# A transformer step on one Trainium2 core: the first stage loads x by tokens, turns it on TensorE, and has its order written by hand

## The chip, the cores and the metric

The kernel runs on one core of a Trainium2 chip. The metric is the device time of one execution in microseconds (us), as the median of several runs. The profile is one execution with the hardware profiler on. Engines are named as the profile names them: PE is TensorE (PEld its weight loads), DVE is VectorE, ACT is ScalarE, POOL is GpSimd, SP is SyncE, which here only issues DMAs.

## The reference, cut to what matters

One step of a two-layer model on 384 tokens of width 1024: 128 context tokens and 256 latent tokens. What the change touches is the start of the first layer, up to the attention's values:

```
def rmsnorm(x, g):
    y = xf * lax.rsqrt(jnp.mean(xf * xf, axis=-1, keepdims=True) + EPS)
    return (y * g)
mod = jax.nn.silu(cond) @ w_ada + b_ada        # six vectors: sm, cm, gm, sf, cf, gf
h = modulate(rmsnorm(x, norm_mix_g[l]), sm, cm) # h * (1 + scale) + shift
q, k, v = qkv_proj(h, w_qkv[j])                # here: v = h @ w_v
```

Context and latent tokens have different conditioning vectors, so shift and scale differ between the two groups. After it come keys, queries, attention, the output projection, a gated convolutional FFN, a second layer with a spatial gMLP, and its FFN.

## The kernel before, in words

Activations lie with features on partitions: `x[0..7]` are eight tiles of 128 features by 384 tokens. Each float32 product is made of three products of a rounded and a rest part (`mac`, L101 to L105: hi·hi, lo·hi, hi·lo). The parts of a weight tile `st` are made on ACT (`hi`, a cast) and DVE (`lo`, the difference).

The first stage, "values' stage", begins at the start of the program and ends with the first product of the keys. In it:

- SP loads x as eight pieces of 128x384 (L66), already turned on the host; then per feature block k two tiles `adw` of modulation weights (512 KB each) and a tile `st` of value weights (512 KB). `adw` has four buffers, `st` three.
- ACT squares each piece of x, DVE adds them up (`square`, L267 to L272), PE sums over partitions (`sums`, L284), DVE and POOL make r = 1/rms (`rsqrt`), and PE spreads r over the partitions into `R` (`rms`, L302).
- `ada_block(k)` (L145 to L157) makes shift and scale of feature block k: 16 small products into a bank, a copy on ACT to `ada_sb`, a turn by PE (L151), three small steps on DVE.
- `modulated` (L328 to L332) makes block k of h in two parts: `u` (named t384, shown as t) = x·scale·R on DVE, `hhi` on ACT, `hlo` on DVE, each for 128 and then 256 tokens.
- Per block k, 18 products of 128x512 add V into six banks `acc`, one for each half of the width and each of three blocks of tokens.

```
        acc = [bank(q) for q in (ps_mm, ps_mm, ps_mm, ps_sc, ps_sc, ps_ta)]
        for k in range(KD):
            modulated(0, SM, CM, k, R)
            w = load(w_v[k])
            if k < KD - 1:
                ada_block(k + 1)
```

PE starts with 18 products of a tile of ones, which nothing reads (L80). In this stage a scheduler sets the order of instructions on each engine. Behind it (from L580 to L663 of the function `attention`) the order of PE, ACT, DVE and SP is the one in which the code is written; from the fifth output tile on a scheduler sets it again.

Of the kernel before, what the change touches and what calls it, by code (L numbers as in the profile page):

```python
# [8 lines left out]
F32 = mybir.dt.float32  # L9
# [6 lines left out]
P = 128  # L16
# [23 lines left out]
def backbone(ctx: ExitStack, tc: tile.TileContext, xT_in, cond_in, condr_in, b_ada_in, prm_in,  # L40
# [17 lines left out]
    def bank(pool):  # L58
        return pool.tile([P, 512], F32, name="bank", tag="bank")


    cond = cst.tile([P, KD, 2], F32, name="cond")
    nc.gpsimd.dma_start(cond, cond_in)
    x = [cst.tile([P, NT], F32, name=f"x{k}") for k in range(KD)]
# [4 lines left out]
    nc.scalar.activation(zero, zero, AF.Silu)  # L69
    cond_s = cst.tile([P, KD, 32], F32, name="cond_s")  # L70
    nc.vector.memset(cond_s, 0.0)
    nc.scalar.activation(cond_s[:, :, 0:2], cond, AF.Silu)
# [49 lines left out]
    def ada_load(f):  # L122
# [7 lines left out]
    w_first = ada_load(0)  # L130
    b_ada = cst.tile([P, 2, 48], F32, name="b_ada")
    nc.sync.dma_start(b_ada, b_ada_in)
    prm = cst.tile([P, NPRM], F32, name="prm")
    nc.sync.dma_start(prm, prm_in)

    def ada_block(f, tpool=ps_tb):


        pa = bank(ps_ad)
        w = ada_load(f) if f else w_first  # L140
# [9 lines left out]
        tp = bank(tpool)  # L150
# [144 lines left out]
    def rms(ss=None, pin=False):  # L295

        if ss is None:
            ss = sums()
        r = inverse(ss)
        R = bank(ps_tb)  # L300
        for b in range(3):
            mm = nc.tensor.matmul(R[:, b * P:(b + 1) * P], r[:, b:b + 1].to_broadcast([P, P]), ident,  # L302
                                  start=True, stop=True)
            if pin and b == 0:
                tc.keep_in_program_order(mm)
        return R
# [64 lines left out]
    def h(k, s=slice(0, NT)):  # L371
        return hhi[:, k, s], hlo[:, k, s]
# [15 lines left out]
    def attention(pool, wkp):  # L388
# [23 lines left out]
        acc = [bank(q) for q in (ps_mm, ps_mm, ps_mm, ps_sc, ps_sc, ps_ta)]  # L412
        for k in range(KD):
            modulated(0, SM, CM, k, R)
            w = load(w_v[k])
            if k < KD - 1:
                ada_block(k + 1)
            for half in range(2):
                for b in range(3):
                    mac(acc[3 * half + b], h(k, slice(b * P, (b + 1) * P)),  # L420
                        wsel(w, half, slice(0, 512)), k == 0, k == KD - 1)
        for b in range(3):
            for half in range(2):
                nc.scalar.copy(V[:, b, 512 * half:512 * half + 512], acc[3 * half + b])
        nc.gpsimd.dma_start(sv_out, V[:, 0, :])

        allm = slice(0, P)
# [134 lines left out]
        def values(t, pT, pool=ps_mm):  # L562
# [11 lines left out]
            for hh in range(2):  # L574
# [5 lines left out]
        order = tc.manual_schedule(engines={mybir.EngineType.PE, mybir.EngineType.Activation,  # L580
                                            mybir.EngineType.DVE, mybir.EngineType.SP})
        order.__enter__()
# [5 lines left out]
        ready()  # L588
        p = products()
        ready()  # L590
# [72 lines left out]
        order.__exit__(None, None, None)  # L663
# [185 lines left out]
def _layout(inp):  # L849
# [8 lines left out]
    xT = xx.T.reshape(KD, P, NT).transpose(1, 0, 2)  # L858
# [8 lines left out]
    def units(w):  # L867
# [9 lines left out]
        "xT": xT, "cond": cond, "condr": np.stack([A["c_ctx"], A["c"][0]]),  # L877
# [39 lines left out]
```

## Time and profile before

| | |
|---|---|
| median of 3 runs | 1020.77 us (1020.12 to 1022.55) |
| profiled execution, its own time | 1021.07 us |
| its span in the trace | 1019.3 us |
| PE busy | 997.6 us, 98% of the span |
| DVE, ACT, POOL busy | 775.9, 482.0, 14.7 us |
| mean granted clock of PE | 0.991 of full speed |
| mean DMA rate | 170 GB/s |

The span runs from the first to the last instruction of the trace; the execution's own time is 1.8 us longer. Busy shares are averages over the whole program: what a change to the first stage can bring is read from that stage alone.

### The profile page before, as it was taken

To read this page: it belongs to the slowest core of one execution; us is meant where nothing else is said; L and a number is where in the kernel's file an instruction comes from. 1 tells how busy PE (TensorE), PEld (TensorE's weight loads), DVE (VectorE), ACT (ScalarE), POOL (GpSimd) and SP (SyncE) were. 2 spreads that over 40 slices of the span, in tenths; PEclk is the share of its full clock that TensorE was granted. 3 is DMA by queue.
4 is the path that set the end of the run, shared out by engine and by line. 5 is a ranking of instruction groups with operands and counts; after the bars stand their busy time and mean duration, and the time that the engine had idled before them with its cause. 6 is when DMAs were issued, how large, how long until landed. Compare 5 with 4: busy or idle time off the path is not lost.

```text
span 1019.3 us, 15937 instructions
## 1 busy us (share of the span) xinstructions
PE 997.6 (98%) x6012; PEld 947.1 (93%) x6012; DVE 775.9 (76%) x1591; ACT 482.0 (47%) x841; POOL 14.7 (1%) x29
## 2 busy tenths in 40 slices
PE   7999999999999999999999999999999999999996
PEld 6788788789999999999998889999999999999996
DVE  3646666568999898999989999688598777776652
ACT  3446555557655555433354434343385444443331
POOL 1000000000000000000000000000000000000000
PEclk7999999999999999999999999999999999999998
DMA  7874646624465555576737765565325434435521
GB/s 261 303 251 147 211 153 220 230 83 146 136 191 169 165 147 159 149 240 203 227 116 258 240 210 154 172 206 187 104 84 166 144 124 125 124 114 172 159 72 62
DMA packets 53933, 172.96 MB, mean 170 GB/s; under 512 B 6225, under 2 KB 12513, under 8 KB 53857
## 3 DMA queue, kind: packets, MB, share of 16 engines
q1 hardware_dynamic: 52992, 170.11, 51.8%
q8 instruction: 47, 0.77, 0.3%
q0 software_dynamic: 432, 1.06, 0.3%
q10 hardware_dynamic: 432, 0.79, 0.2%
q14 instruction: 30, 0.24, 0.1%
HBM read 169.31 MB, written 2.62 MB: 169 GB/s over the span
## 4 chain that ended last, share of the span: by engine, by line
PE 91%; DMA 3%; DVE 2%; ACT 2%; issue 1%; POOL 0%; SPq 0%; POOLq 0%; ACTq 0%; DVEq 0%
PE bank L103 28%; PE bank L105 28%; PE bank L104 28%; DMA kT<-in_ckT 2%; PE bank L145 1%; PE bank L788 1%; PE bank L568 1%; PE bank L519 1%; PE bank L190 1%; PE bank L551 1%; DMA adw<-in_w_ada 1%; PE bank L284 1%; ACT pr L536 0%; DMA cond<-in_cond 0%; PE bank L302 0%
## 5 line engine op out<-in xcount | busy, mean ns | idle before, releaser
L96 ACT CAST hi<-st 128x1024 fp32r<-128x1024 f32 (+1 forms) x192 | 198.1, 1033 | 300.6 <-PE bank L104 239.0
L105 PE MATMUL bank<-hhi,lo 128*128 128x384 f32 (+1 forms) x960 | 325.2, 339 | 0.2 <-DVE lo L109 0.2
L104 PE MATMUL bank<-hlo,hi 128*128 128x384 f32 (+1 forms) x960 | 324.7, 338 | 0.0
L103 PE MATMUL bank<-hhi,hi 128*128 128x384 f32 (+1 forms) x960 | 324.6, 338 | 0.0
L97 DVE TENSOR_TENSOR lo<-st,hi 128x1024 fp32r<-128x1024 f32 (+1 forms) x192 | 230.0, 1199 | 66.4 <-ACT hi L96 66.1
L105 PEld LDWEIGHTS bank<-hhi,lo 128*128 128x128 f32 x960 | 181.1, 189 | 0.5 <-DVE lo L109 0.5
L103 PEld LDWEIGHTS bank<-hhi,hi 128*128 128x128 f32 x960 | 181.0, 189 | 0.4 <-ACT kT L475 0.2
L104 PEld LDWEIGHTS bank<-hlo,hi 128*128 128x128 f32 x960 | 180.4, 188 | 0.1
L248 DVE CUSTOM_DVE_ANT_0 junk<-adw,cs 128x1024 bf16<-128x1024 f32 x112 | 136.6, 1219 | 1.0
L105 PE MATMUL bank<-ahi,lo 128*128 128x384 f32 x352 | 118.9, 338 | 0.0
L104 PE MATMUL bank<-alo,hi 128*128 128x384 f32 x352 | 118.9, 338 | 0.0
L103 PE MATMUL bank<-ahi,hi 128*128 128x384 f32 x352 | 118.7, 338 | 0.0
L105 PEld LDWEIGHTS bank<-ahi,lo 128*128 128x128 f32 x352 | 66.1, 188 | 0.0
L104 PEld LDWEIGHTS bank<-alo,hi 128*128 128x128 f32 x352 | 66.1, 188 | 0.0
L103 PEld LDWEIGHTS bank<-ahi,hi 128*128 128x128 f32 x352 | 66.1, 188 | 0.0
L103 PE MATMUL bank<-hi,hhi 128*128 128x512 f32 x144 | 58.2, 408 | 1.8 <-ACT hhi L330 1.8
L104 PE MATMUL bank<-lo,hhi 128*128 128x512 f32 x144 | 57.4, 398 | 0.0
L105 PE MATMUL bank<-hi,hlo 128*128 128x512 f32 x144 | 57.3, 399 | 0.0
L376 DVE SCALAR_TENSOR_TENSOR x<-bank,mod,x 128x128 f32<-128x128 f32 x64 | 23.8, 412 | 34.4 <-PE bank L105 34.2
L103 PE MATMUL bank<-mhi,hi 128*128 128x384 f32 x128 | 43.3, 339 | 0.0
L105 PE MATMUL bank<-mhi,lo 128*128 128x384 f32 x128 | 43.2, 337 | 0.0
L104 PE MATMUL bank<-mlo,hi 128*128 128x384 f32 x128 | 43.1, 337 | 0.0
(154 smaller groups left out, 1265.5 us busy)
## 6 DMA issues: line engine op xcount, KB each, us to landing
st<-in_w_up SPq DMA_DIRECT2D x88, 512.0 KB, 3.6
adw<-in_w_adaT SPq DMA_DIRECT2D x56, 512.0 KB, 4.2
adw<-in_w_ada SPq DMA_DIRECT2D x40, 512.0 KB, 5.6
st<-in_w_down SPq DMA_DIRECT2D x32, 512.0 KB, 3.6
st<-in_w_qk SPq DMA_DIRECT2D x16, 512.0 KB, 3.7
st<-in_w_gu SPq DMA_DIRECT2D x16, 512.0 KB, 4.3
st<-in_w_gv SPq DMA_DIRECT2D x16, 512.0 KB, 4.5
st<-in_w_gout SPq DMA_DIRECT2D x16, 512.0 KB, 4.5
```

What stands on the lines that cost most here:

```text
L96: nc.scalar.copy(hi[:, :n], st[:, :n])
L97: nc.vector.tensor_tensor(lo[:, :n], st[:, :n], hi[:, :n].bitcast(F32), ALU.subtract)
L103: nc.tensor.matmul(out, a[0], b[0], start=start, stop=False)
L104: nc.tensor.matmul(out, a[0], b[1], start=False, stop=False)
L105: nc.tensor.matmul(out, a[1], b[0], start=False, stop=stop)
L145: nc.tensor.matmul(pa[32 * j:32 * j + 32, 0:P], cond_s[:, 4 * hf + kk, :], w[hf][:, kk, P * q:P * q + P], start=(kk == 0), stop=(kk == 3), ...
L190: nc.tensor.matmul(self.pa[32 * j:32 * j + 32, 0:256], cond_s[:, k, :], t[:, 256 * j:256 * j + 256], start=(k == 0), stop=(k == KD - 1), t ...
L248: tc.keep_in_program_order(nc.vector.tensor_tensor_reduce(self.junk, t, self.cs[c], 1.0, 0.0, ALU.mult, ALU.add, m[:, c:c + 1]))
L284: mm = nc.tensor.matmul(ss[:, 2 * b:2 * b + 2], src[:, b * P:(b + 1) * P], ones[:, 0:2], start=(i == 0 and b == 0), stop=(i == len(srcs) - ...
L376: nc.vector.scalar_tensor_tensor(x[m][:, a:b], ps[:, a:b], mod(l, gate, m, c), x[m][:, a:b], ALU.mult, ALU.add)
L519: nc.tensor.matmul(sc[hh][:, cols], q[qp][HS[hh], qs:qs + P], k[kp][HS[hh], ks], start=i == 0, stop=i == 2)
L551: nc.tensor.transpose((ta[:, o:o + P] if g < 2 else tb[:, o - 512:o - 512 + P]), pr[:, b, g * P:g * P + P], ident)
```

## The change

- x comes as three tiles of 128 tokens by 1024 features (`xs`, in three buffers of the pool of `lo` tiles, which the order rows name `lo`). The first and third are issued by SP, the second by ACT. PE turns them (`turn_x`, 24 turns of 128x128 into the banks of `acc`), ACT and DVE copy the eight results to `x[k]` (`copy_x`).
- The sum of squares is taken along each token's row, by one instruction for each tile (ACT twice, DVE once); `sums` is not called here any more. R is used from its bank for block 0 and copied afterwards.
- `b_ada` and `prm` (small parameter tiles) are loaded by POOL in place of SP, behind `cond` and before `ident` is made.
- The second pair of `adw` tiles (`late=True`) is first touched by a memset on DVE, placed behind the last step of r; its loads wait for that, and the loads behind them in SP's queue too. Later pairs are issued three blocks ahead.
- PE is given 8 products of a constant bfloat16 tile `fill` at the start in place of the 18 of ones, one more behind each tile's turns, 4 before R and 5 before the first product of V (`busy`).
- The whole stage is under the written order. In block k, the weights of block k+1 are split at the start of the step; the modulation products of block k+1 stand behind the first of six groups of three products, and their turn behind the second.
- The last block's products stand behind the first loads of the keys' stage, and V's six copies out are shared: four on ACT and two on DVE.

```diff
+    xs = [wlp.tile([P, D], F32R, name="lo", tag="lo").bitcast(F32) for _ in range(3)]
+    for b in range(3):
+        (nc.sync, nc.scalar)[b % 2].dma_start(xs[b], x_in[b])
-    for k in range(KD):
-        nc.sync.dma_start(x[k], xT_in[:, k, :])
-    warm = bank(ps_ad)
-    for _ in range(18):
-        nc.tensor.matmul(warm[:, :P], ones, ones, start=True, stop=True)
+            if late:
+                nc.vector.memset(st[:, 0:1], 0.0)
-        for k in range(KD):
-            square(k, ("t384", "t384", "R0")[k % 3])
-        ss = sums(True)
-        ada_block(0, ps_ta)
-        Rp = rms(ss, True)
+        aw = {0: ada_load(0)}
+        st = [v_load(0)]
+        busy(8, idle)
+        for b in range(3):
+            if b == 1:
+                nc.vector.tensor_tensor_reduce(jv, xs[b], xs[b], 1.0, 0.0, ALU.mult, ALU.add, ssq[:, b:b + 1])
+            else:
+                nc.scalar.activation(junk, xs[b], AF.Square, accum_out=ssq[:, b:b + 1])
+            for k in range(6):
+                turn_x(k, acc[k], (b,))
+            busy(1, idle)
+        r = rsqrt(ssq[:, 0:3], tmp.tile([P, 4], F32, name="rv", tag="rv", bufs=2)[:, 0:3], 1.0 / D)
+        aw[1] = ada_load(1, True)
+        st.append(v_load(1))
+        for k in range(6):
+            copy_x(k, acc[k])
+        busy(4, idle)
+        Rp = spread(r)
+        sb = ada_products(aw.pop(0))
+        aw[2] = ada_load(2)
+        st.append(v_load(2))
+        for k in (6, 7):
+            turn_x(k, acc[k - 2], range(3))
+        w = v_high(st.pop(0))
+        ada_turned(0, sb, acc[5][:, NT:512])
+        shaped(0, Rp, lambda: v_low(w, 0, 512))
...
+        v_low(w, 512, 1024)
+        busy(5, acc[3])
+        for k in range(KD - 1):
+            if k:
+                w2 = v_high(st.pop(0))
+                v_low(w2)
+            v_part(k, w, parts[:1])
+            sb = ada_products(aw.pop(k + 1))
+            if k + 3 < KD:
+                aw[k + 3] = ada_load(k + 3)
+                st.append(v_load(k + 3))
+            v_part(k, w, parts[1:2])
+            ada_turned(k + 1, sb, bank(ps_tb))
+            if not k:
+                w2 = v_high(st.pop(0))
+            shaped(k + 1, R, None if k else lambda: v_low(w2))
+            v_part(k, w, parts[2:])
+            w = w2
```

PE, from its start to the second block of modulation products, before (`ones` is the tile of ones; a name's number is the buffer's):

```order
L80 MATMUL bank<-ones 128x128 x18
L284 MATMUL bank<-ones,sqacc 128x2 x3
L284 MATMUL bank<-ones,t_213 128x2 x3
L145 MATMUL bank<-adw,cond_s 32x128 x16
L151 MATMUL bank<-ident,ada_sb 128x128
L302 MATMUL bank<-ident,rr 128x128 x3
L103 MATMUL bank<-hi,hhi 128x512 x2
L145 MATMUL bank<-adw,cond_s 32x128 x2
L103 MATMUL bank<-hi,hhi 128x512 x2
L104 MATMUL bank<-lo,hhi 128x512
```

PE after the change, from the turns of the third tile of x (`lo` is that tile) to the same place; the rows left out are fills:

```order
L449 MATMUL bank<-ident,lo 128x128 x6
L417 LDWEIGHTS fill
L417 MATMUL bank<-fill 128x512
...
L310 MATMUL bank<-ident,rr 128x128 x3
L150 MATMUL bank<-adw,cond_s 32x128 x16
L449 MATMUL bank<-ident,lo 128x128 x6
L158 MATMUL bank<-ident,ada_sb 128x128
...
L112 MATMUL bank<-hi,hhi 128x512
L113 MATMUL bank<-lo,hhi 128x512
L114 MATMUL bank<-hi,hlo 128x512
L150 MATMUL bank<-adw,cond_s 32x128 x16
```

The sums over partitions are gone, R now stands ahead of the first modulation products, six turns of x stand between those and their own turn, and the first V group is complete (hi·hi, lo·hi, hi·lo) before the next modulation block.

DVE before, from the first step of r to the first `hlo`:

```order
L311 TENSOR_SCALAR rv<-bank 128x3
L315 TENSOR_TENSOR rt<-ry 128x3
L316 SCALAR_TENSOR_TENSOR rt<-rt,rv 128x3
L318 SCALAR_TENSOR_TENSOR rr<-rt,ry 128x3
L154 TENSOR_TENSOR mod_143<-bank,b_ada 128x2x2
L157 TENSOR_TENSOR mod_143<-mod_143,bank 128x2x2
L117 SCALAR_TENSOR_TENSOR mod_143<-mod_143,prm 128x2
L328 SCALAR_TENSOR_TENSOR t_267<-x_93,mod_143,R_259 128x128
L328 SCALAR_TENSOR_TENSOR t_267<-x_93,mod_143,R_259 128x256
L97 TENSOR_TENSOR lo<-st,hi 128x1024
L332 SCALAR_TENSOR_TENSOR hlo<-t_267,mod_143,hhi 128x128
```

DVE after, from the last step of r on:

```order
L324 SCALAR_TENSOR_TENSOR rr<-rt,ry 128x3
L137 MEMSET adw 128x1 x2
L452 COPY x_99<-bank 128x384
L452 COPY x_101<-bank 128x384
L452 COPY x_103<-bank 128x384
L161 TENSOR_TENSOR mod_129<-bank,b_ada 128x2x2
L164 TENSOR_TENSOR mod_129<-mod_129,bank 128x2x2
L126 SCALAR_TENSOR_TENSOR mod_129<-mod_129,prm 128x2
L438 SCALAR_TENSOR_TENSOR t_289<-x_99,mod_129,bank 128x128
L438 SCALAR_TENSOR_TENSOR t_289<-x_99,mod_129,bank 128x256
L432 TENSOR_TENSOR lo<-st,hi 128x512
L444 SCALAR_TENSOR_TENSOR hlo<-t_289,mod_129,hhi 128x128
```

The two memsets that release the second pair of `adw` loads, and three copies of x, now stand between r and the modulation, and only the first half of `lo` stands ahead of `hlo`.

SP before, from the last piece of x:

```order
L66 DMA x_100<-in_xT 128x384
L127 DMA adw<-in_w_ada 128x1024 x2
L132 DMA b_ada<-in_b_ada 128x96
L134 DMA prm<-in_prm 128x408
L93 DMA st<-in_w_v 128x1024
L127 DMA adw<-in_w_ada 128x1024 x2
L93 DMA st<-in_w_v 128x1024
```

SP after, from its start (`lo` are the first and third tile of x):

```order
L71 DMA lo<-in_x 128x1024 x2
L139 DMA adw<-in_w_ada 128x1024 x2
L421 DMA st<-in_w_v 128x1024
L139 DMA adw<-in_w_ada 128x1024 x2
L421 DMA st<-in_w_v 128x1024
```

Eight pieces became two on this queue, the small parameters left it, and the fourth row here waits for DVE's memsets, with everything behind it.

## Rows read from the trace of the kernel before

**Rows 1.** The page, part 1: busy time and share of the span, instructions.

```profile
PE 997.6 (98%) x6012; PEld 947.1 (93%) x6012; DVE 775.9 (76%) x1591; ACT 482.0 (47%) x841; POOL 14.7 (1%) x29
```

**Rows 2.** Stretch by engine: length, busy time (count) each, granted clock, DMA share, GB/s.

```profile
18.00:65.00 47.00, 46.98 (x375) 34.03 (x376) 25.64 (x61) 19.86 (x36) 0.27 (x1) 0.94 0.75 259
```

**Rows 3.** Timeline of 0 to 25 us: start, length, engine, line, operation.

```profile
1.36 6.95 PE L80 MATMUL bank<-ones 128*128 128x128 f32 x36 [1.36 <-DVE mhalf L82]
...
5.37 3.65 ACT L270 ACTIVATE t<-x 128x384 f32<-128x384 f32 x7
...
12.13 0.16 DVE L311 TENSOR_SCALAR rv<-bank 128x3 f32<-128x3 f32 x1 [2.34 <-PE bank L284]
...
13.82 0.16 DVE L318 SCALAR_TENSOR_TENSOR rr<-rt,ry 128x3 f32<-128x3 f32 x1
...
14.46 0.45 PE L151 MATMUL bank<-ident,ada_sb 128*128 128x128 f32 x1 [0.50 <-ACT ada_sb L149]
...
14.70 1.50 PE L302 MATMUL bank<-ident,rr 128*128 128x128 f32 x6
...
15.33 0.16 DVE L117 SCALAR_TENSOR_TENSOR mod<-mod,prm 128x2 f32<-128x2 f32 x1
16.24 0.48 ACT L411 COPY R<-bank 128x384 f32<-128x384 f32 x1 [1.92 <-PE bank L302]
...
18.02 1.22 PE L103 MATMUL bank<-hi,hhi 128*128 128x512 f32 x2 [1.82 <-ACT hhi L330]
```

**Rows 4.** Stretches of half a us, columns as in Rows 2.

```profile
6.50:7.00 0.50, 0.50 (x4) 0.50 (x4) 0.42 (x1) 0.44 (x2) 0.00 (x0) 1.00 1.47 350
7.00:7.50 0.50, 0.50 (x7) 0.50 (x6) 0.40 (x2) 0.50 (x2) 0.00 (x0) 1.00 0.81 264
...
10.50:11.00 0.50, 0.50 (x4) 0.50 (x4) 0.00 (x0) 0.00 (x0) 0.00 (x0) 0.50 1.09 423
...
24.50:25.00 0.50, 0.50 (x5) 0.44 (x4) 0.10 (x1) 0.50 (x1) 0.00 (x0) 1.00 1.54 131
```

**Rows 5.** Timeline of PE, two modulation blocks and the stage's end.

```profile
44.43 1.08 PE L145 MATMUL bank<-adw,cond_s 128*32 128x128 f32 x32
...
49.91 1.08 PE L145 MATMUL bank<-adw,cond_s 128*32 128x128 f32 x32
...
64.79 0.39 PE L105 MATMUL bank<-hi,hlo 128*128 128x512 f32 x1
65.02 0.34 PE L103 MATMUL bank<-hhi,hi 128*128 128x384 f32 x1
```

**Rows 6.** Groups by line and shape, 0 to 60 us: count, busy us, mean ns.

```profile
L97 DVE TENSOR_TENSOR lo<-st,hi 128x1024 fp32r<-128x1024 f32 x8 | 9.8, 1222 | 1.2 <-ACT hi L96 1.1
L96 ACT CAST hi<-st 128x1024 fp32r<-128x1024 f32 x8 | 8.4, 1048 | 0.2 <-DMA st<-in_w_v 0.2
...
L330 ACT ACTIVATE hhi<-t,mod 128x128 fp32r<-128x128 f32 x8 | 3.3, 406 | 6.5 <-DVE t L328 6.5
...
L328 DVE SCALAR_TENSOR_TENSOR t<-x,mod,R 128x128 f32<-128x128 f32 x8 | 2.8, 352 | 1.5 <-ACT R L411 1.3
```

**Rows 7.** The same view for ACT, 60 to 180 us.

```profile
L536 ACT ACTIVATION_READ_ACCUMULATOR pr<-bank,st 128x1 f32 x28 | 5.5, 198 | 0.0
```

**Rows 8.** A stretch of 5 us, columns as in Rows 2.

```profile
10.00:15.00 5.00, 4.50 (x47) 3.93 (x48) 0.78 (x5) 0.27 (x1) 1.57 (x4) 0.54 1.03 414
```

**Rows 9.** Tiles adw, then x, 0 to 75 us: issue to landing.

```profile
DMA to landing us min/median/max: 3.4/5.7/8.8
DMA to landing us min/median/max: 2.5/4.1/4.2
```

**Rows 10.** Stretches of 1 us at the program's end, columns as in Rows 2.

```profile
1010.00:1011.00 1.00, 1.00 (x11) 1.00 (x10) 0.10 (x1) 0.00 (x0) 0.75 (x1) 1.00 0.00 0
...
1013.00:1014.00 1.00, 0.00 (x0) 0.00 (x0) 0.86 (x2) 0.58 (x2) 0.00 (x0) 0.96 0.61 233
```

**Rows 11.** Timeline of PE at the program's end: x turned back.

```profile
1009.76 1.84 PE L834 MATMUL bank<-ident,x 128*128 128x128 f32 x15
```

More of the change, by code (lines that the diff above doesn't have):

```diff
@@ L59, in bank @@
         return pool.tile([P, 512], F32, name="bank", tag="bank")
+    written = tc.manual_schedule(engines={mybir.EngineType.PE, mybir.EngineType.Activation,
+                                          mybir.EngineType.DVE, mybir.EngineType.SP})
+    written.__enter__()
+    xs = [wlp.tile([P, D], F32R, name="lo", tag="lo").bitcast(F32) for _ in range(3)]
+    for b in range(3):
+        (nc.sync, nc.scalar)[b % 2].dma_start(xs[b], x_in[b])
+    x = [cst.tile([P, NT], F32, name=f"x{k}") for k in range(KD)]
     cond = cst.tile([P, KD, 2], F32, name="cond")
     nc.gpsimd.dma_start(cond, cond_in)
-    x = [cst.tile([P, NT], F32, name=f"x{k}") for k in range(KD)]
-    for k in range(KD):
-        nc.sync.dma_start(x[k], xT_in[:, k, :])
+    b_ada = cst.tile([P, 2, 48], F32, name="b_ada")
+    nc.gpsimd.dma_start(b_ada, b_ada_in)
+    prm = cst.tile([P, NPRM], F32, name="prm")
+    nc.gpsimd.dma_start(prm, prm_in)
     zero = cst.tile([P, 1], F32, name="zero")
@@ L69, in backbone @@
     nc.scalar.activation(zero, zero, AF.Silu)
+    fill = cst.tile([P, 512], BF16, name="fill")
+    nc.vector.memset(fill, 1.0)
     cond_s = cst.tile([P, KD, 32], F32, name="cond_s")
     nc.vector.memset(cond_s, 0.0)
-    nc.scalar.activation(cond_s[:, :, 0:2], cond, AF.Silu)
     ident = cst.tile([P, P], F32, name="ident")
@@ L120, in gain, with ada_load @@
             ALU.add, ALU.mult)
-    def ada_load(f):
+    def ada_load(f, late=False):
         w = []
@@ L128, in ada_load, with ada_products @@
         return w
[L130 to L136, printed above, removed]
+    def ada_products(w):
         pa = bank(ps_ad)
-        w = ada_load(f) if f else w_first
         for kk in range(4):
@@ L293, in inverse, with rms, spread @@
         return rsqrt(ss[:, 0:6].rearrange("p (b c) -> p b c", c=2)[:, :, 0], v[:, 0:3], 1.0 / D)
[L295 to L299, printed above, removed]
+    def rms():
+        return spread(inverse(sums()))
+    def spread(r):
         R = bank(ps_tb)
@@ L403, in attention, with busy, v_load @@
         olo = [pool.tile([P, NT], F32R, name=f"olo{t}") for t in range(NPAIR)]
-        for k in range(KD):
-            square(k, ("t384", "t384", "R0")[k % 3])
-        ss = sums(True)
-        ada_block(0, ps_ta)
-        Rp = rms(ss, True)
+        acc = [bank(q) for q in (ps_mm, ps_mm, ps_mm, ps_sc, ps_sc, ps_ta)]
+        idle = bank(ps_ad)
+        def busy(n, o):
+            for _ in range(n):
+                nc.tensor.matmul(o, fill[:, 0:P], fill, start=True, stop=True)
+        def v_load(k):
+            st = stg.tile([P, 1024], F32, name="st", tag="st")
+            nc.sync.dma_start(st, w_v[k])
+            return st
@@ new lines, in v_high, with v_low, shaped @@
+        def v_high(st):
+            hi = whp.tile([P, 1024], F32R, name="hi", tag="hi")
+            lo = wlp.tile([P, 1024], F32R, name="lo", tag="lo")
+            nc.scalar.copy(hi, st)
+            return st, hi, lo
+        def v_low(w, a=0, b=1024):
+            st, hi, lo = w
+            nc.vector.tensor_tensor(lo[:, a:b], st[:, a:b], hi[:, a:b].bitcast(F32), ALU.subtract)
+        def shaped(k, R, between=None):
+            u = tmp.tile([P, NT], F32, name="t384", tag="t384", bufs=2)
+            for c, a, b in GROUPS:
+                nc.vector.scalar_tensor_tensor(u[:, a:b], x[k][:, a:b], mod(0, CM, k, c),
+                                               R[:, a:b], ALU.mult, ALU.mult)
+                nc.scalar.activation(hhi[:, k, a:b], u[:, a:b], AF.Identity, bias=mod(0, SM, k, c))
+            if between is not None:
+                between()
+            for c, a, b in GROUPS:
+                nc.vector.scalar_tensor_tensor(hlo[:, k, a:b], u[:, a:b], mod(0, SM, k, c),
+                                               hhi[:, k, a:b].bitcast(F32), ALU.add, ALU.subtract)
@@ new lines, in turn_x, with copy_x @@
+        def turn_x(k, o, bs):
+            for b in bs:
+                nc.tensor.transpose(o[:, b * P:b * P + P], xs[b][:, k * P:k * P + P], ident)
+        def copy_x(k, o):
+            (nc.scalar.copy if k % 2 else nc.vector.tensor_copy)(x[k], o[:, :NT])
+        aw = {0: ada_load(0)}
+        st = [v_load(0)]
+        busy(8, idle)
+        ssq = tmp.tile([P, 4], F32, name="ssq", tag="ssq")
+        junk = whp.tile([P, D], F32R, name="hi", tag="hi").bitcast(F32)
+        for b in range(3):
+            if b == 1:
+                jv = whp.tile([P, D], F32R, name="hi", tag="hi").bitcast(F32)
+                nc.vector.tensor_tensor_reduce(jv, xs[b], xs[b], 1.0, 0.0, ALU.mult, ALU.add, ssq[:, b:b + 1])
[4 more added lines that the diff above has]
+            busy(1, idle)
@@ L422, in attention, with v_part @@
[L422 to L425, printed above, removed]
+        for k in (6, 7):
+            copy_x(k, acc[k - 2])
+        v_low(w, 512, 1024)
+        busy(5, acc[3])
+        def v_part(k, w, parts):
+            hl = [p.rearrange("p (a b) -> p a b", b=D) for p in w[1:]]
+            for half, b in parts:
+                mac(acc[3 * half + b], h(k, slice(b * P, (b + 1) * P)),
+                    (hl[0][:, 0, 512 * half:512 * half + 512], hl[1][:, 0, 512 * half:512 * half + 512]),
+                    k == 0, k == KD - 1)
@@ new lines, in v_out @@
+        def v_out(half):
+            for b in range(3):
+                (nc.scalar.copy if b != 1 else nc.vector.tensor_copy)(
+                    V[:, b, 512 * half:512 * half + 512], acc[3 * half + b])
+        parts = [(half, b) for half in range(2) for b in range(3)]
+        for k in range(KD - 1):
[14 more added lines that the diff above has]
+            w = w2
@@ L588, in attention @@
         ready()
+        v_part(KD - 1, w, parts[:3])
+        v_out(0)
+        v_part(KD - 1, w, parts[3:])
+        ready()
+        v_out(1)
+        nc.gpsimd.dma_start(sv_out, V[:, 0, :])
         p = products()
-        ready()
         K = keys(0, kT, p)
@@ L662, in attention @@
                 ready()
-        order.__exit__(None, None, None)
+        written.__exit__(None, None, None)
         for m in range(4, KD):
```

24 lines of the change are left out of this document (5 added, 19 removed).

## The prediction

> **What bounds the kernel now.** I read the page first: PE is busy 98% of the span [rows 1], so only PE work that goes, or time in which PE waits or runs slowly, can pay. The orders of before and after differ only up to the first product of the keys, so I read the timeline up to there. The reader should see two things in it. First, PE gets to its first product of V at 18.02 us, and the chain that leads there does not run through PE's throughput: squares on ACT until 9.02, sums, r from 12.13 to 13.98, the spread of R from 14.70 to 16.20, R's copy, u, hhi [rows 3]. Second, the stretches of half a us show the clock. [...]
>
> The stage's V part runs from 18.02 to 65.02, 47.0 us, at a mean clock of 0.94 [rows 2, 3, 5]. At full clock a step of k takes 5.5 us (44.43 to 49.91), and three products that follow each other 0.69 (0.23 each, 64.79 to 65.02) [rows 5]. Seven steps with a modulation block and one of 18 bare products would be 7 x 5.48 + 18 x 0.23 = 42.5 us. So the half clock costs 4.5 us in V, and the chain ahead of it 18.0 us, of which little is PE work. That is what the change can win from: 22 us, no more.
>
> **The change, part by part.** I follow the chain at full clock, and price the half clock below.
>
> *x lands.* No row shows x in three tiles. Lower bound: the shortest landing of a 192 KB piece was 2.5 us [rows 9], from an issue near 0.7; the other 1.38 MB at the 414 GB/s which weights reached once the queue was full [rows 8] are 3.3 us more: 6.5. Upper bound: as in before, where the last of ACT's seven squares (0.52 each) began at 8.5 [rows 3], so that its piece was there. I take 7.1, nearer the lower end, since the tiles are 4 KB rows like the weights'. That the second tile is on ACT's queue and the others on SP's shares the same rate out in another way; only the last landing counts here. Moving b_ada and prm to POOL delays `ident` by two issues, but it is needed with the first tile only.
>
> *Squares.* Last tile on ACT: 1.05 for 1024 columns [rows 6] plus 0.20 to read the sum [rows 7]: 8.4. The 3.1 us from the last square to r's first step (9.02 to 12.13 [rows 3]) are gone.
>
> *r.* Same steps, 1.85 us (12.13 to 13.98) [rows 3]: 10.3.
>
> *R.* 1.50 us at the half clock [rows 3], so 0.75: 11.0. No R copy ahead of block 0 (0.48 less).
>
> *Modulation products.* 1.08 us [rows 5]: 12.1. Six turns of x stand behind them, at 0.12 each [rows 11]: 12.8. The other 18 turns and the fills lie in the wait for x and r, if the clock is up.
>
> *Turn and three DVE steps.* 14.46 to 15.49 in before [rows 3]; the turn is 0.2 shorter at full clock: 13.65. The copies of x (some 0.5 each, like R's [rows 3]) are done by then.
>
> *u and hhi.* 0.35 + 0.41 [rows 6] and 0.1 of handoff: the first product of V at **14.5**, 3.5 us earlier. Its second product waits for half of `lo` (0.61 of the 1.22 us [rows 6], behind both parts of u), its third for `hlo`: about 0.5 us lost in the first group.
>
> *The V part.* 42.5 us, all at full clock. The weights' parts are ready a step ahead, and the turn stands 0.7 us behind the products, which covers the copy of 128 columns between them (ACT casts 1024 in 1.05 [rows 6]). ACT casts the next weights ahead of that copy, so a late `st` would hold up copy, turn and hhi behind it; in steady steps each `st` is issued some 8 us ahead (two steps of 5.5 less the products and two issues), against a median landing of 5.7 for the tiles beside it [rows 9]. V's copies go out beside the last nine products (2.1 us), and the keys' first bank is free by then.
>
> *Held-back loads.* The second pair is issued after r, at about 10.5 and 10.9. The shortest landing is 3.4, and a second 512 KB takes 1.25 us more at 414 GB/s [rows 8, 9]: 14.9. It is needed at about 15.7, behind the first group. Cost nothing, with 0.8 us of cover; the longest landing of before, 8.8 [rows 9], would uncover 4 us.
>
> Sum: 14.5 + 0.5 + 42.5 = 57.5 in place of 65.02, 7.5 us less. I take off 0.6 for handoffs of the new order that no row shows: 6.9. The profiled execution took 1021.07, so 1014.2; the median is 0.3 lower, **1013.9**.
>
> [...] At the program's end 15 turns run in 1.84 us [rows 11], and the clock was full while almost nothing else was on PE (1010 to 1011) and stayed so until near the end of 1013 to 1014, two us after the last turn [rows 10]. So by these rows turns keep the upper level. [...]
>
> **The rivals.**
>
> *1. The clock falls in the new wait.* PE still waits for x and r, and a fall costs as in before: R, modulation products and six turns at half pace (0.75 + 1.0 + 0.7 = 2.4 us), and up to 4.5 us in V. For it: it fell in before during just this chain [rows 4]. Against it: fills and turns now fill the waits which were empty. The gain would be 0 to 4.5 us: 1016.3 to 1020.8.
>
> *2. The clock never rises before V: slower.* Place: PE's queue, if turns and fills do less for the clock than the 18 products did. At half pace the 15 fills up to R take 0.46 each and the 18 turns 0.24 (doubled): 8 fills end at 5.0, all turns and fills of x at 12.5, R at 14.0, modulation at 16.0, six turns at 17.4, the turn at 17.9, five more fills at 20.2. V would start 2.2 us later than before and lose the same 4.5 us behind it, and 0.5 in the first group: 1021.07 + 2.7, less 0.3, 1023.5. It decides if the clock is still low when R is spread. For it: the fills are now part of the path, which the 18 old ones weren't. Against it: PE is busy from 1.3 on, like in before, where that sufficed by 7.0 [rows 4].
>
> *3. The held-back loads are late.* If the second pair takes the 8.8 us, PE stands 4 us behind the first group, and the loads behind it on SP come later too: gain 2.9, 1017.9 (more if the clock falls there). Against it: that landing was seen where the queue was full.
>
> *4. x lands no earlier than before* (8.5): the first product at 15.9, gain 5.5, 1015.3. This lies in my own case's range.
>
> **How the numbers follow.** Chances: my case, with rival 4 as its upper part, 0.65 (x landing at 6.5 to 8.5 moves the time by -0.6 to +1.4, and the handoffs by up to 0.6 either way; not both ends at once: 1012.6 to 1015.6); rival 1 0.13; rival 2 0.08; rival 3 0.09; other losses 0.05. The range 1012.6 to 1018.4 holds the first, the third and half of the first rival, 0.80. A measurement of this kernel can tell about 0.3%, 3.1 us, from no change, that is a time below 1017.7: 0.65 and half of rivals 1 and 3 and of the rest, 0.78. Slower by as much (above 1023.8): half of rival 2, and little else, 0.05. The same: 0.17.
>
> **What would show it.** In the profile after: the first product of V near 14.5 and the first product of the keys near 57.5; granted clock 1.00 in every stretch from 11 to 57; the square of the third tile starting at about 7.1 and r done by 10.5; the second pair of modulation products not waiting on a load; a step of 5.5 us. Wrong would be: a fall of the clock between 8 and 18 (rival 1), fills at 0.46 up to 12 and a first product near 20 (rival 2), PE waiting on `adw` behind its first V group (rival 3), or steps longer than 5.5, which no part of this working foresees.

## The result, and the profile after

The changed kernel took 1012.44 us (median of 4 runs, 1011.21 to 1013.11) against 1021.66 us (4 runs, 1020.12 to 1023.38): a ratio of 0.9914, with a 95% interval of 0.9895 to 0.9933. The profiled execution took 1011.21 us with a span of 1009.4, where before's span was 1019.3. So the sign and the size came as forecast (1013.9), and the median lies 0.2 us below the lower end of the stated range. In the two profiled executions, whose spans differ by 9.9 us, two things made that up: the stage gave 6.7 us, nearly what was predicted for it, and 3.2 us more came from places that the change does not touch. Of these 3.2 only a part comes back in other executions, as shown below.

PE's share of the span is what it was [rows 1], with less busy time, as part 1 of the profile's page shows for the kernel after:

```profile
PE 991.1 (98%) x6007; PEld 940.8 (93%) x6008; DVE 778.3 (77%) x1597; ACT 479.8 (48%) x839; POOL 15.8 (2%) x31
```

The timeline of the first stage answers to [rows 3] (start, length, engine, line; L417 are the fills, L449 the turns of x, L310 the spread of R, L150 the modulation products, L112 to L114 the products of V):

```profile
1.49 3.59 PE L417 MATMUL bank<-fill 128*128 128x512 bf16 x8 [1.49 <-DVE fill L83]
...
5.81 1.51 PE L449 MATMUL bank<-ident,lo 128*128 128x128 f32 x6 [0.72 <-DMA lo<-in_x]
...
7.29 1.06 ACT L464 ACTIVATE hi<-lo 128x1024 f32<-128x1024 f32 x1 [0.45 <-DMA lo<-in_x]
7.54 1.49 PE L449 MATMUL bank<-ident,lo 128*128 128x128 f32 x6
...
9.24 0.90 PE L449 MATMUL bank<-ident,lo 128*128 128x128 f32 x6
...
9.98 1.24 PE L417 MATMUL bank<-fill 128*128 128x512 bf16 x5
10.18 0.16 DVE L324 SCALAR_TENSOR_TENSOR rr<-rt,ry 128x3 f32<-128x3 f32 x1
...
11.06 0.83 PE L310 MATMUL bank<-ident,rr 128*128 128x128 f32 x6
...
11.82 1.08 PE L150 MATMUL bank<-adw,cond_s 128*32 128x128 f32 x32
...
13.54 0.27 PE L158 MATMUL bank<-ident,ada_sb 128*128 128x128 f32 x1
...
15.10 0.68 DVE L432 TENSOR_TENSOR lo<-st,hi 128x512 fp32r<-128x512 f32 x1
15.28 0.50 PE L112 MATMUL bank<-hi,hhi 128*128 128x512 f32 x1 [0.38 <-ACT hhi L440]
...
15.84 0.50 PE L113 MATMUL bank<-lo,hhi 128*128 128x512 f32 x1
```

What to see: the third square starts at 7.29, as soon as x's last tile is there; r is done at 10.34; and then PE, not r, is late. Six turns of x take 1.5 us in the first two groups and 0.9 in the third, so by this pace the clock rose only at about 9.3 (the column of the granted clock doesn't show it: it reads 1.00 here from the start, as in before ahead of its first fall). The five fills ahead of R hold PE until 11.06, 0.7 us after r was ready. The first product of V starts at 15.28, and the second waits until 15.84 for the low part of the weights.

The stretch from there to the first product of the keys (columns as in [rows 2], to which this row answers) is shorter and has no half clock in it:

```profile
15.28:58.32 43.04, 42.98 (x376) 32.82 (x376) 27.15 (x64) 19.53 (x36) 0.00 (x0) 1.00 0.83 294
```

Two modulation blocks and the stage's end, from PE's timeline, answer to [rows 5]:

```profile
22.01 1.08 PE L150 MATMUL bank<-adw,cond_s 128*32 128x128 f32 x32
27.48 1.08 PE L150 MATMUL bank<-adw,cond_s 128*32 128x128 f32 x32
...
58.09 0.39 PE L114 MATMUL bank<-hi,hlo 128*128 128x512 f32 x1
58.32 0.34 PE L112 MATMUL bank<-hhi,hi 128*128 128x384 f32 x1
```

A step takes 5.5 us, and the keys begin at 58.32 in place of 65.02: 6.7 us. Behind this point the kernel before ran 954.3 us, the changed one 951.1. The largest piece of that difference is in the two FFNs' down projections, 528 products of 128x384 each, which no edit touches. In before the first of them starts at 418.74 and the product after the last at 511.66:

```profile
418.74 0.34 PE L103 MATMUL bank<-ahi,hi 128*128 128x384 f32 x1
...
511.66 0.34 PE L103 MATMUL bank<-hhi,hi 128*128 128x386 f32 x1
```

and in the kernel after:

```profile
411.42 0.34 PE L112 MATMUL bank<-ahi,hi 128*128 128x384 f32 x1
...
502.94 0.34 PE L112 MATMUL bank<-hhi,hi 128*128 128x386 f32 x1
```

92.92 us became 91.52: 176.0 ns from product to product became 173.3. The second FFN repeats it, so 2.8 us are here. This comes back in the second profile of the changed kernel; the whole of the 3.2 does not, for there the part behind the keys took 954.1 us, about as long as in before. The changed program has one more small tile, `ssq`, in the pool `tmp`, which takes 32 bytes of every partition. Together with the other new buffers it puts `ahi` and `alo`, the operands that these products stream, on addresses that are a multiple of 64 bytes, where in before they lie 32 bytes beside one (by the addresses that the two programs allot; no trace shows them). That was the first theory to test.

### The profile page after: what moved, and what is told of

Same layout as the page of the kernel before. It is cut to its first block, busy times and chain, and to the rows that moved or that the text cites. A ratio compares the mean times of both kernels' runs of the same rounds, so it can differ in the third digit from the quotient of the medians.

```text
span 1009.4 us, 15920 instructions
## 1 busy us (share of the span) xinstructions
PE 991.1 (98%) x6007; PEld 940.8 (93%) x6008; DVE 778.3 (77%) x1597; ACT 479.8 (48%) x839; POOL 15.8 (2%) x31
## 4 chain that ended last, share of the span: by engine, by line
PE 92%; DMA 3%; DVE 2%; ACT 1%; issue 1%; POOL 0%; POOLq 0%; SPq 0%; ACTq 0%
PE bank L113 28%; PE bank L114 28%; PE bank L112 28%; DMA kT<-in_ckT 1%; PE bank L883 1%; PE bank L661 1%; PE bank L644 1%; PE bank L612 1%; PE bank L150 1%; PE bank L197 1%; DMA adw<-in_w_ada 1%; DMA lo<-in_x 0%; PE bank L449 0%; POOL ry L319 0%; PE bank L291 0%
## 5 line engine op out<-in xcount | busy, mean ns | idle before, releaser
L105 ACT CAST hi<-st 128x1024 fp32r<-128x1024 f32 (+1 forms) x184 | 189.3, 1030 | 296.2 <-PE bank L113 237.6
L114 PE MATMUL bank<-hhi,lo 128*128 128x384 f32 (+1 forms) x960 | 325.0, 339 | 0.2 <-DVE lo L118 0.2
L112 PE MATMUL bank<-hhi,hi 128*128 128x384 f32 (+1 forms) x960 | 324.6, 338 | 0.0
L106 DVE TENSOR_TENSOR lo<-st,hi 128x1024 fp32r<-128x1024 f32 (+1 forms) x184 | 220.1, 1198 | 64.6 <-ACT hi L105 64.5
L114 PEld LDWEIGHTS bank<-hhi,lo 128*128 128x128 f32 x960 | 181.1, 189 | 0.5 <-DVE lo L118 0.5
L112 PEld LDWEIGHTS bank<-hhi,hi 128*128 128x128 f32 x960 | 181.0, 189 | 0.4 <-ACT kT L568 0.2
L114 PE MATMUL bank<-ahi,lo 128*128 128x384 f32 x352 | 118.3, 336 | 0.0
L112 PE MATMUL bank<-ahi,hi 128*128 128x384 f32 x352 | 118.1, 336 | 0.0
L114 PEld LDWEIGHTS bank<-ahi,lo 128*128 128x128 f32 x352 | 66.2, 188 | 0.0
L112 PEld LDWEIGHTS bank<-ahi,hi 128*128 128x128 f32 x352 | 66.2, 188 | 0.0
L112 PE MATMUL bank<-hi,hhi 128*128 128x512 f32 x144 | 58.1, 403 | 0.4 <-ACT hhi L440 0.4
L114 PE MATMUL bank<-hi,hlo 128*128 128x512 f32 x144 | 56.7, 394 | 0.0
L112 PE MATMUL bank<-mhi,hi 128*128 128x384 f32 x128 | 43.3, 338 | 0.0
L114 PE MATMUL bank<-mhi,lo 128*128 128x384 f32 x128 | 43.3, 338 | 0.0
```

The source lines that it names most:

```text
L105: nc.scalar.copy(hi[:, :n], st[:, :n])
L106: nc.vector.tensor_tensor(lo[:, :n], st[:, :n], hi[:, :n].bitcast(F32), ALU.subtract)
L112: nc.tensor.matmul(out, a[0], b[0], start=start, stop=False)
L114: nc.tensor.matmul(out, a[1], b[0], start=False, stop=stop)
```

## The experiments

Four groups of runs each shared a chip and its runs of the kernel before: the 32 bytes, the changed kernel again and the fills in the kernel before; the three with no fills, loads not held and the late split; the early split and the padded rows; the moved wait (two kernels) and the 64 bytes. Ratios are to before on the same chip, with their 95% intervals. No kernel leaves out any of the computation.

### Where the buffers lie: three kernels, and the changed kernel again

Before, with a pad (the second time 16 wide in place of 8):

```
+    nc.gpsimd.memset(tmp.tile([P, 8], F32, name="pad", tag="pad"), 0.0)
```

The changed kernel without the new 32 bytes:

```
-        ssq = tmp.tile([P, 4], F32, name="ssq", tag="ssq")
+        ssq = tmp.tile([P, 4], F32, name="ssq", tag="rv", bufs=2)
```

Expected of before with 32 bytes: 

> The kernel before, with one unused tile of 32 bytes a partition put into pool tmp, so that every buffer behind it, those of the FFN's hidden values ahi and alo among them, lies 32 bytes further on. No instruction of the first stage changes but one small POOL memset. Theory (placement: the 3.2 us that the changed kernel gained after the values' stage come from where the buffers lie): the products of w_down of both FFNs stand 173.3 ns apart in place of 176.0, so some 2.8 us less over their 1056 products, and the whole is 2 to 4 us faster than before (ratio 0.996 to 0.998); first product of V at 18.0 and first product of the keys at 65.0 as before. Rival (the gain behind the stage belongs to the changed first stage, or differs from program to program for another reason): 176.0 stays and the time is that of before within 0.5 us.

Expected of the changed kernel without them: 

> The changed kernel with its small tile ssq put into a buffer that pool tmp has already, so that the buffers behind tmp lie where those of before lay (relative to 64 bytes). Theory (placement): the products of w_down go back to 176.0 ns apart; the time is 2 to 4 us above that of the changed kernel, 1014.5 to 1016.5, and of the 9.2 us gained only the stage's 6.7 are left; first product of the keys at 58.3 as in the changed kernel. Rival (not placement): 173.3 ns and 1012.4 stay.

Expected of the changed kernel again: 

> The changed kernel again, beside the others on one chip. Both theories: 1012.4 within 1 us, first product of V at 15.3, first product of the keys at 58.3, w_down's products 173.3 ns apart.

Expected of before with 64 bytes: 

> The kernel before with an unused tile of 64 bytes a partition in pool tmp in place of one of 32: the buffers behind tmp move by 64 bytes. Theory (what counts is the address within 64 bytes): the products of w_down stand 176.0 ns apart as in before, and each FFN's down projection takes 93.1 us. Rival (any shift, or the distance to the weights' buffers, changes the pace): 173.3 ns and 91.7 us as with 32 bytes, or a third value.

Measured: the pad alone made before faster, 1017.70 us, ratio 0.9975 (0.9959 to 0.9990). The changed kernel lost by being put back, 1014.41 us, 0.9948 (0.9928 to 0.9968), where on the same chip it had 1012.32 us, 0.9922 (0.9903 to 0.9941). These two intervals overlap, so that the times alone hardly tell the two kernels apart; the pace does. Timeline of PE at the down projection's ends, before with 32 bytes (91.52 us):

```profile
420.64 0.34 PE L104 MATMUL bank<-ahi,hi 128*128 128x384 f32 x1
...
512.16 0.34 PE L104 MATMUL bank<-hhi,hi 128*128 128x386 f32 x1
```

and the changed kernel without them (92.92 us):

```profile
409.53 0.34 PE L112 MATMUL bank<-ahi,hi 128*128 128x384 f32 x1
...
502.45 0.34 PE L112 MATMUL bank<-hhi,hi 128*128 128x386 f32 x1
```

So 32 bytes switch the pace of these products between 176.0 and 173.3 ns, in either kernel: for them, placement sets it. With 64 bytes (one run, 1022.57 us) the stretch took 93.28 us, 176.7 ns a product: slow as in before, if not to the digit.

```profile
419.64 0.34 PE L104 MATMUL bank<-ahi,hi 128*128 128x384 f32 x1
...
512.92 0.33 PE L104 MATMUL bank<-hhi,hi 128*128 128x386 f32 x1
```

The pads lie behind the weights' buffers, which stay where they were, and move `ahi` and `alo`; for these the address within 64 bytes fits the five profiles read at both ends of the stretch: 173.3 ns on a multiple of 64, 176.0 to 176.7 ns 32 bytes beside one. A general rule it is not. `mhi` and `mlo`, the operands of the gMLP's output projection, move by the same 32 bytes onto multiples of 64, and there the pad costs: the 384 products took 67.49 us in before,

```profile
659.75 0.42 PE L103 MATMUL bank<-mhi,hi 128*128 128x384 f32 x1
...
727.24 0.34 PE L103 MATMUL bank<-hhi,hi 128*128 128x386 f32 x1
```

and 67.90 with the 32 bytes:

```profile
660.14 0.42 PE L104 MATMUL bank<-mhi,hi 128*128 128x384 f32 x1
...
728.04 0.34 PE L104 MATMUL bank<-hhi,hi 128*128 128x386 f32 x1
```

### The same idea for the modulated x

The changed kernel with an early split (below), and besides it:

```
-    hhi = hp.tile([P, KD, NT + 2], F32R, name="hhi")
-    hlo = hp.tile([P, KD, NT + 2], F32R, name="hlo")
+    hhi = hp.tile([P, KD, 400], F32R, name="hhi")[:, :, :NT + 2]
+    hlo = hp.tile([P, KD, 400], F32R, name="hlo")[:, :, :NT + 2]
```

with pads of 32 bytes in `cst` and `tmp`, which put the first row on a multiple of 64.

> The version before this one with the rows of the modulated x's high and low parts (hhi, hlo) made 1600 bytes apart in place of 1544 and their first byte put on a multiple of 64. Theory (placement: a moving operand that begins on a multiple of 64 bytes is streamed at 173.3 ns a product, others at 175 to 181): all products that take hhi or hlo as their moving operand, some 3000 of 128 x 384, come down from a mean of 175.6 to 173.3 to 174 ns, 4 to 7 us in all, 1004 to 1008. Rival (the pace of w_down's products has another cause): the mean stays, and the time is that of the version before it within 0.7 us.

Measured: 1012.68 us, 0.9918 (0.9902 to 0.9934), against 1011.03 us without it. The theory falls for these operands. From the end of the first down projection to the start of the second, which is mostly such products, it took 403.7 us, and 403.1 without the padding. So "multiples of 64 are fast" is no rule for every operand. The weights' buffers moved too here, onto multiples of 64: the down projection kept its 91.52 us, while the gMLP's output projection went from the changed kernel's 67.91 to 67.47, with `mhi` and `mlo` on multiples of 64 in both. The moving operand's address is not all that counts; what else does is open.

### The fills, taken away

```
         def busy(n, o):
-            for _ in range(n):
+            for _ in range(0):
```

This takes out all fills, which are 20 (the expectation miscounts them).

> The changed kernel without its 19 fill products; the turns of x, the spread of R and the products of the modulation stay. Theory (the fills carry the clock through the waits for x and r): PE is nearly idle until x lands at 5 us, and the clock is still at its lower level, 0.50, when R is spread and when V begins, so that the products of the first steps run at half pace: V's part 45 to 47.5 us, first product of the keys at 60.5 to 63, the whole 2 to 5 us slower than the changed kernel (1014.5 to 1017.5). Rival (the turns of x alone raise and hold the clock, and the fills ahead of R only stand in its way): R up to 0.8 us earlier, first product of V at 14.5 to 15.3, the time 1011.5 to 1012.5.

Measured: 1011.70 us, 0.9908 (0.9893 to 0.9923): no different from the changed kernel. Both theories were half right, as PE's timeline shows:

```profile
5.62 3.92 PE L449 MATMUL bank<-ident,lo 128*128 128x128 f32 x18 [5.62 <-DMA lo<-in_x]
10.20 0.93 PE L310 MATMUL bank<-ident,rr 128*128 128x128 f32 x6 [0.65 <-DVE adw L137]
...
14.52 0.49 PE L112 MATMUL bank<-hi,hhi 128*128 128x512 f32 x1 [1.46 <-ACT hhi L440]
```

PE did nothing until x landed, and then only turns, 18 in 3.9 us, at half pace. Yet R behind them ran at full pace (0.93 us for six passes; 1.50 at the half clock [rows 3]): with nothing but turns ahead of it the clock had risen. R then comes 0.86 us earlier than in the changed kernel, since no fill is in its way, and V begins at 14.52. But with no fills in the next wait of 1.46 us the clock fell just after 16, by the granted clock of half a us (column as in [rows 2]):

```profile
15.50:16.00 0.50, 0.50 (x10) 0.26 (x13) 0.50 (x2) 0.21 (x1) 0.00 (x0) 1.00 1.08 434
16.00:16.50 0.50, 0.50 (x20) 0.50 (x16) 0.50 (x2) 0.00 (x0) 0.00 (x0) 0.59 1.09 451
16.50:17.00 0.50, 0.50 (x17) 0.49 (x12) 0.24 (x1) 0.00 (x0) 0.00 (x0) 0.50 0.99 401
```

and was back between 19 and 20. V's part took 44.6 us, and the keys began at 59.12, 0.8 us later than in the changed kernel, too little for these runs to resolve. With the fills ahead of V the clock stayed at 1.00 (the row of 15.28 to 58.32 above), worth some 1.5 us in V; what those ahead of R are worth no run shows by itself, and in the changed kernel's profile R stood behind them for 0.7 us.

### The fills alone, in the kernel before

```
-    for _ in range(18):
-        nc.tensor.matmul(warm[:, :P], ones, ones, start=True, stop=True)
...
+    more(24, warm)
...
+        idle = bank(ps_mm)
+        more(4, idle)
         Rp = rms(ss, True)
+        more(9, idle)
```

> The kernel before with its 18 products of ones made 24, and 13 more of them put into the two waits ahead of V: 4 ahead of the spread of R and 9 behind it. Nothing else moves and no buffer. Theory (most of the stage's gain is the half clock that the waits ahead of V cost): the granted clock is 1.00 from 8 to 65, V's part takes 42.5 to 43.0 us in place of 47.0, R and the modulation products are up to 1.5 us earlier, and the whole is 4 to 6 us faster than before (1015 to 1017). Rival (the gain comes from x's turns and the order by hand, the clock falls all the same or the fills stand in the way): V's part stays above 46 and the time within 1 us of before.

Measured: 1018.72 us, 0.9988 (0.9975 to 1.0001), far less than expected. Its profiled execution (1017.87 us) did what the theory said in the stage, V at the full clock and the keys at 60.26 in place of 65.02:

```profile
17.42:60.26 42.84, 42.84 (x373) 32.30 (x372) 24.93 (x59) 19.55 (x35) 0.31 (x1) 1.00 0.80 284
```

So the clock is worth 4.2 us in V and 0.6 ahead of it (not quite by itself: the scheduler also put PE's first products of V in another order). Some 1.5 of these 4.8 us were given back later in that execution, where PE waits for the modulation weights of attention's last pair (2.5 us in three waits; 2.4 in before) and the clock fell behind that wait and behind the next one:

```profile
184.00:188.00 4.00, 4.00 (x15) 4.00 (x15) 2.14 (x4) 2.54 (x7) 0.00 (x0) 0.50 0.93 310
210.00:215.00 5.00, 4.47 (x18) 4.50 (x19) 3.97 (x9) 4.53 (x8) 0.00 (x0) 0.69 0.06 7
```

### That later wait moved

In the kernel with the fills alone, and in the changed kernel with an early split, the last pair's modulation products were moved behind the output projection's first products:

```
-            if last:
-                ada.run(3)
-            else:
+            if not last:
                 K = keys(t + 1, kT, p)
...
         output(0, range(6), ps_mm)
+        ada.run(3)
         ready()
```

Expected with the fills alone: 

> The kernel before with the 19 more products of ones of the earlier run, and with the same move of the three modulation blocks in attention's last pair. Theory (of the 4.8 us that those products won in the values' stage a part was given back at that wait, where PE now arrives earlier and the loads don't, and at the half clock behind it): without the wait the gain shows in full, 1012.5 to 1015.5, that is 3 to 6 us below the run with the fills alone (1018.7). Rival (it was given back elsewhere, or the median of the one run was high): 1016 to 1019.

Expected in the changed kernel with an early split: 

> The version with the early split of the first weights, and in attention's last pair the three blocks of modulation products, for whose loads PE waits 1.6 to 2.8 us in every kernel looked at, put behind the output projection's first 18 products and the turns ahead of them. Theory (that wait, and the half clock that follows it in some executions, is bought by nothing): the wait falls from 1.9 us to under 0.3, the granted clock stays 1.00 from 180 to 190, and the time is 2 to 4 us below that of the version without the move (1007 to 1009). Rival (the loads come as late as whatever stands behind them, or the residual's chain waits for the modulation instead): the wait only moves, and the time stays within 0.7 us of 1011.0.

Measured: 1016.95 us, 0.9960 (0.9944 to 0.9976), and 1011.67 us, 0.9906 (0.9880 to 0.9932), the second no different from the version without the move (1011.03, 0.9913). There the rival holds: PE no longer waits for the load, but for ACT's copies behind the turns, as long as before. The longest wait of PE from 172 to 235 us (in total, times, longest) in the second:

```profile
PE bank L644 <- ACT pT L651: 2.2, 1, 2.2
```

The first kernel is less clear. Its time lies in the rival's range too, but its ratio is 0.0028 below that of the fills without the move (0.9988, on another chip), some 2.9 us with an interval of about 2, and in its profile the clock did not fall behind the two waits, though PE waited as long. Whether the move or the execution did that is open.

It taught something else. Its first stage is the same code as that of the fills alone, but in this execution PE waited 0.6 us for weights and 0.5 for ACT's copy, the clock fell at 14, and the fills then stood at half pace in the way of R, whose r was ready at 13.2 (first the clock, columns as in [rows 2], then PE's timeline):

```profile
14.00:15.00 1.00, 1.00 (x7) 1.00 (x6) 0.48 (x3) 0.85 (x1) 0.00 (x0) 0.50 1.03 418
```

```profile
13.90 1.82 PE L81 MATMUL bank<-ones 128*128 128x128 f32 x8
15.51 1.49 PE L305 MATMUL bank<-ident,rr 128*128 128x128 f32 x6
16.79 2.47 PE L81 MATMUL bank<-ones 128*128 128x128 f32 x18
...
19.54 0.50 PE L106 MATMUL bank<-hi,hhi 128*128 128x512 f32 x1
```

V began at 19.54, later than in before, and the keys at 62.39. So the fills alone gain 4.8 us in one execution and 2.6 in another. Before's own stage varies too (65.02, and 64.04 and 65.34 in the padded kernels). How often each happens isn't known from one profile of each.

### Two parts of the change undone

The loads not held back (`aw[1] = ada_load(1)`), and the split of the next weights put back from the head of a step to its middle:

```
-            if k:
-                w2 = v_high(st.pop(0))
-                v_low(w2)
...
+            w2 = v_high(st.pop(0))
+            shaped(k + 1, R, lambda: v_low(w2))
```

Expected of the loads: 

> The changed kernel with the second pair of modulation weights not held back until r: it is issued as soon as SP comes to it. Theory (the holding back is worth nothing, since SP's queue is in order and x, the first pair and the first weights are issued ahead of it anyway): x lands as before at 4.9 to 6.0, the first product of V at 15.3 and of the keys at 58.3, the time within 0.5 us of 1012.4. Rival (the second megabyte shares the rate with x and with the first weights): x's last tile lands 0.5 to 2.5 us later, and the first product of V, the keys and the end come later by as much.

Expected of the split: 

> The changed kernel with the split of a step's next weights (cast on ACT, subtraction on DVE) taken back from the step's head to within the modulated step, between the high and the low parts, as block 1 has it. Theory (a step is bound by PE, its waits hidden either way): steps of 5.5 us stay, the first product of the keys at 58.3, the time within 0.5 us of 1012.4. Rival (the early split is a part of the gain): PE waits for the low part at the head of steps 2 to 7, 0.3 to 0.6 us each, and the time is 2 to 4 us longer.

Measured: 1011.31 us, 0.9897 (0.9875 to 0.9919), and 1012.37 us, 0.9920 (0.9900 to 0.9941); keys at 57.81 and 58.53. Neither part is worth anything that can be measured. With the loads not held back x landed 4.6, 4.9 and 6.1 us after its issues (shortest, median, longest), in the changed kernel 4.9, 5.2 and 6.0.

### The first weights split earlier

```
-        busy(4, idle)
+        w = v_high(st.pop(0))
+        v_low(w)
+        busy(1, idle)
         Rp = spread(r)
...
-        w = v_high(st.pop(0))
...
-        shaped(0, Rp, lambda: v_low(w, 0, 512))
+        shaped(0, Rp)
...
-        v_low(w, 512, 1024)
```

> The changed kernel with the first weights split (cast and the whole low part) ahead of the spread of R and of the first modulated block, where ACT and DVE wait anyway, and with one fill product in place of four ahead of R. Theory (in the changed kernel the first product of V is late by the fills that R stands behind, 0.6 us, and its second waits 0.55 us for the low part): R is spread from 10.4 in place of 11.06, the first product of V at 14.6 to 14.8, the second does not wait for the low part, the first product of the keys at 57.0 to 57.4, the whole 0.8 to 1.3 us faster than the changed kernel. Rival (the clock needs these fills): the clock falls to 0.50 between 10 and 15, and the whole is 1 to 4 us slower than the changed kernel.

Measured: 1011.03 us, 0.9913 (0.9894 to 0.9931): the lowest median of all, but not told apart from the changed kernel's. Its timeline:

```profile
10.12 0.93 PE L310 MATMUL bank<-ident,rr 128*128 128x128 f32 x6 [1.58 <-DVE adw L137]
...
12.63 1.23 DVE L432 TENSOR_TENSOR lo<-st,hi 128x1024 fp32r<-128x1024 f32 x1 [1.14 <-ACT hi L427]
...
13.77 0.15 DVE L161 TENSOR_TENSOR mod<-bank,b_ada 128x4 f32<-128x4 f32 x1
...
15.18 0.50 PE L112 MATMUL bank<-hi,hhi 128*128 128x512 f32 x1 [0.96 <-ACT hhi L440]
15.52 0.39 PE L113 MATMUL bank<-lo,hhi 128*128 128x512 f32 x1
```

R comes 0.9 us earlier and the second product no longer waits. But the low part, whose weights landed at about 11.5, now keeps DVE until 13.8, and the modulation's steps behind it start at 13.77 (13.09 without fills), so that the first product of V is as late as it was. It won 0.3 us in V's part (42.70 in place of 43.04), not the earlier start.

## Why the prediction was right, point by point

**x, squares, r.** As predicted: the last tile was there by 7.29 (7.1 said; the DMA queues brought 397 to 430 GB/s from 3 to 6 us, x on two of them, where 414 was taken), the last square's sum was read at 8.45 (8.4), r done at 10.34 (10.3). Rival 4 is out.

**R and the modulation.** Here the chain slipped. R's turn on PE came at 11.06 to 11.82, where the spread was to be done by 11.0, and everything behind carried it: turns of x 12.83 (12.1), the turn 13.54 (12.8), first product of V 15.28 (14.5). I had put turns and fills into the wait for r "if the clock is up", and in this execution it wasn't until 9.3. In its second profile the same kernel ran its first six turns at full pace, R at 10.69 and V from 15.01:

```profile
5.70 0.85 PE L449 MATMUL bank<-ident,lo 128*128 128x128 f32 x6 [0.71 <-DMA lo<-in_x]
```

Over the eight profiles with the changed order and the fills ahead of V, V began between 14.60 and 15.53. The term was mis-sized by some 0.1 to 1.0 us, and the fills ahead of R are a part of it.

**The V part.** 43.0 us forecast (42.5 and 0.5 lost in the first group), 43.04 measured. The first group took 1.25 us, to the modulation products at 16.53, where three products that follow each other take 0.69, so that 0.56 was lost there. V's part was 42.6 to 43.1 in all eight. **The stage** gave 6.7 us for 6.9 forecast: the 0.6 taken off for handoffs, which no row backed, met the slip of 0.8. That the stage's sum came out so near is in part luck.

**The rivals.** Rival 1 did not happen with fills in the wait ahead of V; without them it did. Rival 2 happened half: the first turns ran at half pace, but the clock rose in time. In the kernel with the fills alone and the moved wait, fills did stand at half pace ahead of R (four of them 1.82 us), and V began at 19.54. Rival 3 is out: the second modulation block did not wait, and holding its load back is worth nothing that these runs can measure.

**Two sums.** The held-back pair's 10.5, 3.4 and 1.25 add up to 15.15, not to 14.9; its second tile landed at 15.20, and nothing waited for it. And 0.6 and 0.6 below 1013.9 is 1012.7: the range's lower end of 1012.6 lay already beyond "both ends at once". Neither changes the forecast.

**Turns and the clock.** I had read from the program's end that turns hold the clock, and had no row on whether they raise it. The run without fills has one: 18 turns and nothing else from 5.62 on, and R at full pace from 10.20 (0.93 us for its six passes).

**What was not foreseen.** The sum held the stage alone, and took everything behind it as unmoved. Placement was worth 2.8 us in the down projections (1.4 in each FFN), in either kernel, and 2 to 3 in the medians (2.1 in the changed kernel, 2.9 in before, each give or take 1.5 to 2). Without it the median would have come out inside the range: the changed kernel without the 32 bytes took 1014.41, 6.2 us less than before on its chip (1020.59), where 6.9 were forecast.

**What stays open.** Behind the stage the granted clock differs between executions of like kernels. Before's profiled execution had no fall between its stage and the program's last microseconds; the changed kernel's had one (0.74 from 205 to 210), its second profile two. PE waits at these places in all kernels, and none of the edits here removes the waits. The 14 profiles show what it is worth: from the first product of the keys to the first FFN's down projection they took 350.6 to 353.7 us where the clock did not fall (4 profiles), 352.7 to 354.3 with one fall (4), and 354.7 to 356.9 with two (6). The runs of one kernel differ by up to 8 us, and this clock is a good part of that; what decides whether it falls is open. Effects under 2 us, such as the early split's, stayed unresolved.

## What to carry to other kernels

Where PE is the bound, look for stretches in which it waits and for the granted clock behind them: here the half clock after a wait of a few us cost more (4.0 us in V) than the shorter chain ahead of V gave (2.7). Work put into such a wait must not stand ahead of the instruction that the chain waits for, since at the half clock it takes longer there: four fills took 1.06 us ahead of R in one execution of before with fills, and 1.82 in another. What fills are worth to a whole kernel is less sure than what they are worth to its stage: the changed kernel without any took 1011.70 us, no different from it with them. And compare the pace of products that an edit didn't touch: a new 32-byte tile was worth 2.8 us in the down projections, which looked like this change's gain.

## What the runs showed of the hardware

- The 128x384 products that stream `ahi` and `alo` stood 173.3 ns apart in the changed kernel and in before with 32 bytes, where the programs put those buffers on a multiple of 64 bytes, and 176.0 in before and in the changed kernel without the 32 bytes, 176.7 in before with 64, where they lie 32 bytes beside one. It is no rule for other operands: the gMLP's output projection lost 0.4 us by the same shift of 32 bytes (67.49 us, then 67.90).
- In the run without fills PE's clock rose with turns alone on it: 18 of them in 3.92 us at half pace, nothing ahead of them, and the next products (six passes in 0.93 us, where before's took 1.50) at full pace.
- The clock rose at different times in two executions of one kernel: the changed kernel ran its first turns of x at half pace in one profile (1.51 us for six) and at full pace in another (0.85), behind the same eight fills.
